# Spreading the modulation products over both products of a feed-forward block

## The chip, the cores and the metric

The kernel runs on one core of one Trainium2 chip. The metric is device time in microseconds (us) of one execution. A profile of one execution of the kernel before is read throughout; in it the span is counted from the first to the last instruction of the core.

## What is computed

A two-layer backbone over 256 latent tokens and 256 context tokens of width 1024. Each layer is a SwiGLU feed-forward block, a pair of token mixers, and a second feed-forward block; each of the three is wrapped in norms that are modulated by vectors computed from a conditioning vector:

```python
for l in range(DEPTH):                                   # DEPTH = 2
    mod = (silu(c) @ w_ada[l] + b_ada[l])                # 9 vectors of 1024 for the latent tokens
    mod_c = (silu(c_ctx) @ w_ada[l] + b_ada[l])          # 9 for the context tokens
    x = add_residual(x, swiglu(modulate(x, nw[0], mod[0], mod[1]), ffn_w_in[l, 0], ffn_w_out[l, 0]), nw[1], mod[2], 0.5)
    ...                                                  # the same for the context tokens, then the mixers
    x = add_residual(x, swiglu(modulate(x, nw[4], mod[6], mod[7]), ffn_w_in[l, 1], ffn_w_out[l, 1]), nw[5], mod[8], 0.5)

def swiglu(h, w_in, w_out):                              # w_in 1024 x 5632, w_out 2816 x 1024
    a, b = split(h @ w_in, 2)
    return (silu(a) * b) @ w_out
```

The "modulation products" are the rows of `silu(c) @ w_ada`. In this kernel they aren't matmuls: w_ada lies transposed, and each product is a multiply-and-sum on VectorE.

## The kernel before, in words

All matrix products are done on TensorE as three passes (`mm3`, L280 to L283): each operand is split into a high and a low part (`split`, L112 to L117: a cast on ScalarE, L115, then a subtraction on VectorE, L116), and high x high, high x low and low x high are summed.

A feed-forward block (`ffn`, L288) has two loops. The first product (`fin`) runs over 22 column blocks f of 128 hidden units. For each it loads 1 MB of weights as two tiles `raw` of 512 KB (`load`, L104; issued by SyncE, L108), splits each into a tile `w`, does 8 x 2 x 3 = 48 matmuls (L281 to L283) over 512 token columns, and evaluates silu(a)*b into `g` (`fin_ev`, L305 to L309: ScalarE L307, VectorE L308). The second product (`fout`) runs over 11 pairs of hidden blocks; for each it loads two `raw` tiles again, splits them, splits two `g` tiles into `gs` (L354 and L355), and does 48 matmuls with 512 output columns. In the last feed-forward block only the 256 latent tokens are left.

The modulation products run beside these loops. One step of the generator `ada_gen` (L127 to L137) loads two `raw` tiles of w_ada and does, for each tile and each of the two conditions, one multiply-and-sum on VectorE (L133): four VectorE instructions a step, two where only the latent condition is left. `pump` (L139) takes steps of a chain of such generators. In the first feed-forward block of a layer the chain has 24 steps: a gate (4), a shift and a scale (8), a gate (4), a shift and a scale (8). In the second of layer 0 it has 12, in the last one 4. At the end of a gate, small VectorE instructions (L185, L186) finish it and GpSimd writes it to DRAM (L188, `scr`), from where it is read back later (L194). The conditions silu(c) lie in the tiles `cs`, two of the 15 slots that `g` is taken from too.

Four `raw` tiles exist for all loads: fin, fout and w_ada share them in turn. Five `w` tiles exist, that is two and a half blocks of split weights. The order on each engine is set by a scheduler that goes by the order of the program and by when it expects operands to be ready; SyncE issues its loads in one order, VectorE and ScalarE do theirs in one order, and an instruction that waits holds those behind it on its engine.

In the loop before, the steps are dealt out over the f loop of the first product alone (L333 to L335): 24 steps over 20 f, that is one step behind each f and two behind every fifth.

Of the kernel before, what the change touches and what calls it, by code (L numbers as in the profile page):

```python
# [24 lines left out]
NF = FF // P  # L25
# [7 lines left out]
def build(ctx, tc, a):  # L33
# [34 lines left out]
    slots = Ring(rp, "r", 15)  # L68

    def bank():  # L70
        return banks.get([P, 512])

    def slot(shape, dt=F32):
        return slots.get(shape, dt)
# [4 lines left out]
    def tmp2(shape=(P, 512), dt=F32):  # L79
        return t2.tile(list(shape), dt, tag="t2", name="t2")  # L80
# [23 lines left out]
    def load(src, halves=(0, 1)):  # L104
        rs = []
        for j in halves:
            r = rawp.tile([P, 1024], F32, tag="raw", name="raw")
            nc.sync.dma_start(r, src[:, j * 1024:(j + 1) * 1024])  # L108
            rs.append(r)
        return rs  # L110

    def split(src, pin=False):  # L112
        keep = tc.keep_in_program_order if pin else (lambda z: z)
        w = wp.tile([P, 2, 1024], F32R, tag="w", name="w")
        keep(nc.scalar.copy(w[:, 0, :], src))  # L115
        keep(dve.tensor_tensor(out=w[:, 1, :], in0=src, in1=w[:, 0, :], op=ALU.subtract))  # L116
        return w  # L117

    cs = {}

    def load_cs(conds):
        for c in conds:
            cs[c] = slot([P, D])
            nc.sync.dma_start(cs[c], a["cc"][c].partition_broadcast(P))
            tc.keep_in_program_order(act(cs[c], cs[c], AF.Silu))
# [13 lines left out]
    def pump(g, n=1):  # L139
        for _ in range(n):  # L140
            if next(g, 1) == 1:
                return
# [75 lines left out]
    def norm_xn(c, alloc):  # L218
        xs = []
        for j in range(2):  # L220
            t = 2 * c + j
            ss = small(2, "ss")
            for hf in range(2):
                junk = jp.tile([P, 512], BF16, tag="ja", name="ja")
                act(junk, X[t][:, hf * 512:(hf + 1) * 512], AF.Square, accum_out=ss[:, hf:hf + 1])  # L225
            r = rstd_2(ss)
            xn = alloc([P, D])
            dve.tensor_scalar(out=xn, in0=X[t], scalar1=r, scalar2=None, op0=ALU.mult)
            xs.append(xn)
        return xs  # L230

    def norm_q(c, q, xs, AB, h):
        A, B = AB
        bk = bank()
        b = bk.rearrange("p (k n) -> p k n", k=2)
        for kk in range(2):
            k = 2 * q + kk
            for j in range(2):
                nc.tensor.transpose(b[:, kk, j * P:(j + 1) * P], xs[j][:, k * P:(k + 1) * P], ident)  # L239
        hf = tmp2([P, 2, 256])  # L240
        for kk in range(2):
            k = 2 * q + kk
            act(hf[:, kk, :], b[:, kk, :], AF.Identity, bias=B[:, c, k:k + 1], scale=A[:, c, k:k + 1])
        banks.put(bk)
        hH = h[q][:, :, 0, c * 256:(c + 1) * 256]
        dve.tensor_copy(hH, hf)  # L246
        dve.tensor_tensor(out=h[q][:, :, 1, c * 256:(c + 1) * 256], in0=hf, in1=hH, op=ALU.subtract)
# [32 lines left out]
    def mm3(o, wH, wL, xH, xL, start, stop):  # L280
        mm(o, lhsT=wH, rhs=xH, start=start, stop=False)  # L281
        mm(o, lhsT=wH, rhs=xL, start=False, stop=False)  # L282
        mm(o, lhsT=wL, rhs=xH, start=False, stop=stop)  # L283

    def fin_w(l, i, f, halves=(0, 1), pin=False):
        return [split(r, pin) for r in load(a["fin"][l, i, f], halves)]

    def ffn(l, i, st, AB, fetch, pairs, side, nside, after=None, out=None, xctx=None):  # L288
        h, w01 = st
        NT = 2 * len(pairs)  # L290
        N = 256 * len(pairs)
        g = {}

        def fin_mm(fs, ws, abs_, c0, c1):
            for k in range(KD):
                for f in fs:
                    wt = ws[f][k // 4].rearrange("p s (k n) -> p s k n", k=4)
                    for z in range(2):
                        lw = wt[:, :, k % 4, z * P:(z + 1) * P]
                        mm3(abs_[f][z][:, c0:c1], lw[:, 0], lw[:, 1], h[k // 2][:, k % 2, 0, c0:c1],  # L300
                            h[k // 2][:, k % 2, 1, c0:c1], k == 0, k == KD - 1)

        def fin_ev(f, ab):
            if f % 2 == 0:
                g[f // 2] = slot([P, 2, 512])  # L305
            sg = tmp2()
            act(sg[:, :N], ab[0][:, :N], AF.Silu)  # L307
            dve.tensor_tensor(out=g[f // 2][:, f % 2, :N], in0=ab[1][:, :N], in1=sg[:, :N], op=ALU.mult)  # L308
            banks.put(*ab)  # L309

        f0 = 0
        if len(pairs) == 2:
            if w01 is None:
                w01 = [fin_w(l, i, 0), fin_w(l, i, 1)]
            ab01 = [[bank(), bank()], [bank(), bank()]]
            fin_mm((0, 1), w01, ab01, 0, 256)
            xs = xctx or norm_xn(CTX, tmp4)
            for q in range(4):
                norm_q(CTX, q, xs, AB, h)
            if xctx:  # L320
                slots.put(*xctx)
            fin_mm((0, 1), w01, ab01, 256, 512)
            for f in range(2):
                fin_ev(f, ab01[f])
            f0 = 2
        load_cs(pairs)
        done = 0
        for f in range(f0, NF):
            w = fin_w(l, i, f, pin=False)
            ab = [bank(), bank()]  # L330
            fin_mm((0,), [w], [ab], 0, N)
            fin_ev(f, ab)
            want = (f + 1 - f0) * nside // (NF - f0)  # L333
            pump(side, want - done)
            done = want  # L335
        for _ in side:
            pass
        slots.put(*cs.values())
        cs.clear()

        y = [[bank(), bank()] for _ in range(NT)]
        NP = NF // 2

        def fout_w(f2):
            r = load(a["fout"][l, i, f2])
            ws = [split(r[0]), split(r[1])]
            if f2 < NP - 2:
                gt = hp.tile([P, 2, 2, 512], F32R, tag="h", name="gs")
                gs = [gt[:, 0], gt[:, 1]]
            else:  # L350
                gs = [slot([P, 2, 512], F32R) for _ in range(2)]
            for j in range(2):
                gsrc = g[f2][:, j, :N]
                nc.scalar.copy(gs[j][:, 0, :N], gsrc)  # L354
                dve.tensor_tensor(out=gs[j][:, 1, :N], in0=gsrc, in1=gs[j][:, 0, :N], op=ALU.subtract)  # L355
            slots.put(g[f2])
            return ws, gs

        def fout_mm(t, j, ws, gs, start, stop, halves=(0, 1)):
            gH = gs[j][:, 0, t * P:(t + 1) * P]  # L360
            gL = gs[j][:, 1, t * P:(t + 1) * P]
            for hf in halves:
                cs_ = slice(hf * 512, (hf + 1) * 512)
                mm3(y[t][hf], gH, gL, ws[j][:, 0, cs_], ws[j][:, 1, cs_], start, stop)

        for f2 in range(NP - 2):
            ws, gs = fout_w(f2)
            for j in range(2):
                for t in range(NT):
                    fout_mm(t, j, ws, gs, f2 == 0 and j == 0, False)  # L370
        tail = [fout_w(NP - 2), fout_w(NP - 1)]
        Gb = fetch()
        for t in range(NT):
            for hf in range(2):
                for e in range(2):
                    for j in range(2):
                        fout_mm(t, j, tail[e][0], tail[e][1], False, e == 1 and j == 1, (hf,))
            post_norm(t, y[t], Gb, out)
            if t == 1 and after is not None:
                after()  # L380
        slots.put(*tail[0][1], *tail[1][1], *Gb.values())
# [617 lines left out]
```

## Time and profile before

| | |
|---|---|
| time, median of 3 runs | 2244.57 us (2239.93 to 2246.06) |
| span of the profiled execution | 2238.5 us |
| from the start of the last work in the chain (2234.64 us) to the span's end | 3.9 us |
| PE busy | 2179.3 us (97%) |
| DVE busy | 1377.6 us (62%) |
| ACT busy | 859.2 us (38%) |
| bytes moved | 307.34 MB, mean 137 GB/s |

The profile gives the profiled execution by its span alone; it lies 1.4 us under the fastest and 6.1 us under the median of the timed runs. In the profile, PE is TensorE's matmul, PEld its weight load, DVE is VectorE, ACT ScalarE, POOL GpSimd, SP SyncE; SPq and POOLq are the issues of DMAs. PEclk is the granted TensorE clock as a share of 2.4 GHz. The four feed-forward blocks lie in the trace at about 24 to 413 us (layer 0, first), 945 to 1301 us (layer 0, second), 1315 to 1670 us (layer 1, first) and 2043 to 2235 us (the last).

### The profile page before, as it was taken

The page shows a single profiled execution, that of the slowest core. Times are in us where ns is not written, and L with a number is a line of the kernel's source. Part 1 is how long each engine was busy: PE and PEld are TensorE (multiplying, and loading weights), DVE is VectorE, ACT ScalarE, POOL GpSimd, SP SyncE. Part 2 cuts the span into 40 slices and gives each one's busy share as a digit, 9 for nine tenths or more (in the row PEclk, how much of TensorE's full clock was granted, in tenths as well). Part 3 has the DMA queues.
Part 4 walks back from the last instruction along what each step waited for, and adds up shares of the span by engine and source line. Part 5 has one row for each costly group of instructions (what it writes and reads, how often), then busy time and mean ns, then how long its engine had stood idle before and what let it go on. Part 6 is the DMA issues. An engine that isn't in the chain of part 4 may idle for free. (4 is left out here: it accounts for less than half of the span.)

```text
span 2238.5 us, 32969 instructions
## 1 busy us (share of the span) xinstructions
PE 2179.3 (97%) x13280; PEld 1936.9 (87%) x13280; DVE 1377.6 (62%) x2234; ACT 859.2 (38%) x1379; POOL 134.9 (6%) x249
## 2 busy tenths in 40 slices
PE   7999999999999999999999999999999999998998
PEld 4887778799999999888888888888879999997997
DVE  3786662586767665565644268746338767766564
ACT  3221242555445432432223252223236545445443
POOL 1000000200100000100000020000011000001000
PEclk9999999999999999999999999999999999999999
DMA  7665552122122223255544327667322322445673
GB/s 297 188 225 162 197 170 94 66 79 89 54 88 67 71 91 116 67 169 151 170 141 133 102 69 207 217 203 235 102 68 97 121 80 93 141 142 168 221 216 123
DMA packets 85546, 307.34 MB, mean 137 GB/s; under 512 B 10416, under 2 KB 10544, under 8 KB 85392
## 3 DMA queue, kind: packets, MB, share of 16 engines
q1 hardware_dynamic: 82224, 295.87, 40.7%
q0 software_dynamic: 2880, 8.31, 1.4%
q8 instruction: 104, 1.70, 0.3%
q10 hardware_dynamic: 288, 1.05, 0.1%
q14 instruction: 50, 0.41, 0.1%
HBM read 304.10 MB, written 1.09 MB: 136 GB/s over the span
## 5 line engine op out<-in xcount | busy, mean ns | idle before, releaser
L115 ACT CAST w<-raw 128x1024 fp32r<-128x1024 f32 x408 | 427.4, 1051 | 833.0 <-PE ps L283 470.7
L116 DVE TENSOR_TENSOR w<-raw,w 128x1024 fp32r<-128x1024 f32 x408 | 497.0, 1221 | 399.8 <-ACT w L115 398.9
L283 PE MATMUL ps<-h,w 128*128 128x256 f32 (+1 forms) x2176 | 718.9, 331 | 9.2 <-DVE w L116 9.1
L281 PE MATMUL ps<-h,w 128*128 128x256 f32 (+1 forms) x2176 | 717.5, 331 | 3.7 <-DVE h L246 2.9
L282 PE MATMUL ps<-h,w 128*128 128x256 f32 (+1 forms) x2176 | 718.5, 331 | 0.0
L283 PEld LDWEIGHTS ps<-h,w 128*128 128x128 f32 x2176 | 413.5, 190 | 52.2 <-DVE w L116 12.3
L281 PEld LDWEIGHTS ps<-h,w 128*128 128x128 f32 x2176 | 412.8, 190 | 43.0 <-DVE h L246 4.0
L282 PEld LDWEIGHTS ps<-h,w 128*128 128x128 f32 x2176 | 413.9, 190 | 40.3 <-DVE w L116 0.8
L133 DVE CUSTOM_DVE_ANT_0 jd<-raw,r 128x1024 bf16<-128x1024 f32 x224 | 273.6, 1222 | 161.1 <-DMA raw<-wada_dram 157.8
L281 PE MATMUL ps<-w,h 128*128 128x256 f32 x1088 | 308.9, 284 | 0.0
L282 PE MATMUL ps<-w,h 128*128 128x256 f32 x1088 | 308.1, 283 | 0.0
L283 PE MATMUL ps<-w,h 128*128 128x256 f32 x1088 | 307.8, 283 | 0.0
L281 PEld LDWEIGHTS ps<-w,h 128*128 128x128 f32 x1088 | 208.6, 192 | 0.4
L282 PEld LDWEIGHTS ps<-w,h 128*128 128x128 f32 x1088 | 208.7, 192 | 0.3
L283 PEld LDWEIGHTS ps<-w,h 128*128 128x128 f32 x1088 | 208.6, 192 | 0.0
L281 PE MATMUL ps<-w,gs 128*128 128x512 f32 x504 | 197.4, 392 | 2.5 <-ACT gs L354 2.5
L282 PE MATMUL ps<-w,gs 128*128 128x512 f32 x504 | 197.3, 391 | 0.0
L283 PE MATMUL ps<-w,gs 128*128 128x512 f32 x504 | 197.2, 391 | 0.0
L281 PEld LDWEIGHTS ps<-w,gs 128*128 128x128 f32 x504 | 95.3, 189 | 22.8 <-ACT gs L354 2.9
L283 PEld LDWEIGHTS ps<-w,gs 128*128 128x128 f32 x504 | 95.3, 189 | 20.5 <-DVE gs L355 0.7
L282 PEld LDWEIGHTS ps<-w,gs 128*128 128x128 f32 x504 | 95.3, 189 | 19.7
L307 ACT ACTIVATE t<-ps 128x512 f32<-128x512 f32 (+1 forms) x88 | 47.6, 541 | 115.8 <-PE ps L283 115.8
(166 smaller groups left out, 2131.3 us busy)
## 6 DMA issues: line engine op xcount, KB each, us to landing
raw<-fin_dram SPq DMA_DIRECT2D x176, 512.0 KB, 4.3
raw<-wada_dram SPq DMA_DIRECT2D x128, 512.0 KB, 4.6
raw<-win_dram SPq DMA_DIRECT2D x128, 512.0 KB, 3.6
raw<-fout_dram SPq DMA_DIRECT2D x88, 512.0 KB, 3.6
r<-wada_dram SPq DMA_DIRECT2D x16, 512.0 KB, 10.2
raw<-wout_dram SPq DMA_DIRECT2D x16, 512.0 KB, 3.5
r<-scr POOLq DMA_DIRECT2D x10, 512.0 KB, 4.8
r<-cc_dram SPq DMA_DIRECT2D x7, 512.0 KB, 5.0
```

The costliest lines, as they stand in the source:

```text
L115: keep(nc.scalar.copy(w[:, 0, :], src))
L116: keep(dve.tensor_tensor(out=w[:, 1, :], in0=src, in1=w[:, 0, :], op=ALU.subtract))
L133: dve.tensor_tensor_reduce(out=junk, in0=r[j], in1=cs[c], scale=1.0, scalar=0.0, op0=ALU.mult, op1=ALU.add, accum_out=out[:, c, 2 * u + j: ...
L281: mm(o, lhsT=wH, rhs=xH, start=start, stop=False)
L282: mm(o, lhsT=wH, rhs=xL, start=False, stop=False)
L283: mm(o, lhsT=wL, rhs=xH, start=False, stop=stop)
L307: act(sg[:, :N], ab[0][:, :N], AF.Silu)
```

## The change

The steps of the chain are dealt out over the f loop of the first product and over the first 9 of the 11 pairs of the second, and the chain is drained, and the `cs` slots are given back, behind that second loop. The count per call is rounded up, against a denominator that is two short of the loops' total length less one, so the chain is through one call before the last. For 24 steps there are 29 calls and a denominator of 28, and 18 steps come in the first product and 6 in the second; no call takes two.

```diff
         load_cs(pairs)
-        done = 0
+        NP = NF // 2
+        done = [0, 0]
+
+        def pump_to_here():
+            done[0] += 1
+            want = min(nside, -(-done[0] * nside // (NF - f0 + NP - 3)))
+            pump(side, want - done[1])
+            done[1] = want
+
         for f in range(f0, NF):
             w = fin_w(l, i, f, pin=False)
             ab = [bank(), bank()]
             fin_mm((0,), [w], [ab], 0, N)
             fin_ev(f, ab)
-            want = (f + 1 - f0) * nside // (NF - f0)
-            pump(side, want - done)
-            done = want
-        for _ in side:
-            pass
-        slots.put(*cs.values())
-        cs.clear()
+            pump_to_here()
...
             for j in range(2):
                 for t in range(NT):
                     fout_mm(t, j, ws, gs, f2 == 0 and j == 0, False)
+            pump_to_here()
+        for _ in side:
+            pass
+        slots.put(*cs.values())
+        cs.clear()
         tail = [fout_w(NP - 2), fout_w(NP - 1)]
```

The order of the instructions on TensorE and on GpSimd is the same in both kernels; on ScalarE one cast in each of three feed-forward blocks stands a few places later. VectorE and SyncE are reordered inside the feed-forward blocks only.

On SyncE, in the first product of the first feed-forward block, this stood at the third place where two steps came behind one f (raw are the load tiles, fin_dram the weights of the first product, wada_dram those of the modulation):

```order
L108 DMA raw_1633<-fin_dram 128x1024
L108 DMA raw_1635<-fin_dram 128x1024
L108 DMA raw_1696<-wada_dram 128x1024
L108 DMA raw_1698<-wada_dram 128x1024
L108 DMA raw_1708<-fin_dram 128x1024
L108 DMA raw_1710<-fin_dram 128x1024
L108 DMA raw_1778<-wada_dram 128x1024
L108 DMA raw_1780<-wada_dram 128x1024
L108 DMA raw_1790<-wada_dram 128x1024
L108 DMA raw_1792<-wada_dram 128x1024
L108 DMA raw_1802<-fin_dram 128x1024
L108 DMA raw_1804<-fin_dram 128x1024
```

And this stands in the changed kernel in the same product, some blocks on, at one of the two places where a call takes no step:

```order
L108 DMA raw_1579<-wada_dram 128x1024
L108 DMA raw_1581<-wada_dram 128x1024
L108 DMA raw_1591<-fin_dram 128x1024
L108 DMA raw_1593<-fin_dram 128x1024
L108 DMA raw_1654<-fin_dram 128x1024
L108 DMA raw_1656<-fin_dram 128x1024
L108 DMA raw_1724<-wada_dram 128x1024
L108 DMA raw_1726<-wada_dram 128x1024
L108 DMA raw_1736<-fin_dram 128x1024
L108 DMA raw_1738<-fin_dram 128x1024
```

The four loads of w_ada in a row are gone; loads of the two kinds alternate in pairs, and now and then two pairs of fin follow each other.

On VectorE, at the change from the first to the second product of the first feed-forward block, the order before was (L133 the modulation products, L116 the subtraction for a weight tile w, L308 the end of a block of the first product, L355 the split of g into gs, where two steps' products still stand ahead of it):

```order
L133 ISA jd_2189,adar_362<-raw_2181,r5_612 128x1024
L170 TENSOR_TENSOR adaB_365<-adar_362,bada_99 128x8 x2
L308 TENSOR_TENSOR r1_1937<-ps3_1964,t2_2013 128x512
L116 TENSOR_TENSOR w_2209<-raw_2205,w_2209 128x1024
L355 TENSOR_TENSOR r9_2783<-r1_1937,r9_2783 128x512
L116 TENSOR_TENSOR w_2212<-raw_2207,w_2212 128x1024
L308 TENSOR_TENSOR r2_2088<-ps5_2039,t2_2089 128x512
L116 TENSOR_TENSOR w_2272<-raw_2268,w_2272 128x1024
L355 TENSOR_TENSOR r4_2798<-r2_2088,r4_2798 128x512
L355 TENSOR_TENSOR gs_2215<-r3_602,gs_2215 128x512 x2
L116 TENSOR_TENSOR w_2275<-raw_2270,w_2275 128x1024
```

In the changed kernel the same place reads (L356 is L355 of before):

```order
L116 TENSOR_TENSOR w_2131<-raw_2127,w_2131 128x1024
L356 TENSOR_TENSOR r9_2783<-r1_1871,r9_2783 128x512
L133 ISA jd_2257,adar_363<-raw_2253,r4_609 128x1024
L116 TENSOR_TENSOR w_2134<-raw_2129,w_2134 128x1024
L133 ISA jd_2259,adar_363<-raw_2253,r5_612 128x1024
L308 TENSOR_TENSOR r2_2022<-ps5_1973,t2_2023 128x512
L133 ISA jd_2261,adar_363<-raw_2255,r4_609 128x1024
L116 TENSOR_TENSOR w_2194<-raw_2190,w_2194 128x1024
L133 ISA jd_2263,adar_363<-raw_2255,r5_612 128x1024
L356 TENSOR_TENSOR gs_2137<-r3_602,gs_2137 128x512 x2
L356 TENSOR_TENSOR r3_2798<-r2_2022,r3_2798 128x512
```

The four products of one step (raw_2253 and raw_2255) now stand among the splits of the first weight tiles of the second product (w_2131, w_2134, w_2194) and ahead of its first gs; before, no product came behind the last evaluation but one.

## Rows read from the trace of the kernel before

**Rows 1.** The page's first line on the engines: busy time, share of the span, instructions.

```profile
PE 2179.3 (97%) x13280; PEld 1936.9 (87%) x13280; DVE 1377.6 (62%) x2234; ACT 859.2 (38%) x1379; POOL 134.9 (6%) x249
```

**Rows 2.** What TensorE's matmuls waited for in the whole span: line, releaser, us in total, times, longest.

```profile
PE ps L239 <- DVE t L228: 16.7, 12, 6.2
PE ps L894 <- DMA r<-wada_dram: 10.1, 2, 9.9
PE ps L283 <- DVE w L116: 9.1, 6, 5.0
...
PE ps L281 <- ACT gs L354: 2.5, 1, 2.5
```

**Rows 3.** The same view for 60 to 300 us (first feed-forward block) and for 1339 to 1660 us (the first of layer 1).

```profile
PE ps L283 <- DVE w L116: 7.4, 3, 5.0
...
PE ps L283 <- DVE w L116: 1.2, 1, 1.2
```

**Rows 4.** Busy time by stretch, in the columns of the view (us, then PE, PEld, DVE, ACT, POOL busy with counts, granted clock, DMA share, GB/s): the two stretches of half clock in the first feed-forward block, one behind it, and a like place behind the second block.

```profile
222.60:229.40 6.80, 5.39 (x13) 4.23 (x14) 6.73 (x11) 0.00 (x0) 0.00 (x0) 0.50 0.60 198
297.70:304.50 6.80, 6.46 (x15) 4.64 (x16) 6.80 (x11) 6.80 (x12) 1.12 (x2) 0.50 0.82 256
417.20:420.60 3.40, 3.40 (x15) 3.21 (x16) 1.52 (x4) 2.65 (x6) 0.00 (x0) 0.50 0.00 0
...
936.00:943.00 7.00, 6.52 (x36) 5.38 (x37) 4.21 (x8) 4.40 (x11) 1.64 (x4) 1.00 0.00 0
```

**Rows 5.** The same view by stage: first product of the second block of layer 0; both products of the first block of layer 0, of the second of layer 0, and of the first of layer 1; both of the last block.

```profile
972.00:1189.00 217.00, 217.00 (x958) 179.65 (x958) 125.15 (x177) 61.77 (x73) 2.99 (x4) 1.00 0.51 161
...
66.00:400.00 334.00, 323.97 (x1399) 265.26 (x1398) 212.12 (x315) 86.41 (x105) 4.69 (x6) 0.98 0.55 173
972.00:1287.00 315.00, 315.00 (x1391) 260.80 (x1391) 155.71 (x209) 87.84 (x104) 2.99 (x4) 1.00 0.45 146
1339.00:1656.00 317.00, 315.77 (x1393) 261.13 (x1393) 183.00 (x262) 85.94 (x104) 3.89 (x5) 1.00 0.57 182
2045.00:2221.00 176.00, 176.00 (x1275) 167.56 (x1274) 103.62 (x130) 83.21 (x112) 1.55 (x2) 1.00 0.62 198
```

**Rows 6.** Counts in the first product of the first block: weight splits on VectorE (L116) since 56 us, and last the matmuls since 66 us (us, busy and count, granted clock, DMA share, GB/s).

```profile
56.00:98.00 42.00, 12.22 (x10) 1.00 0.60 199
...
56.00:208.00 152.00, 33.32 (x28) 1.00 0.64 200
56.00:218.00 162.00, 34.16 (x28) 1.00 0.64 195
...
66.00:218.00 152.00, 152.00 (x674) 1.00 0.65 199
```

**Rows 7.** In order of time: VectorE's and SyncE's work from 189 to 201 us, one cycle with one step, then what stands around 207 to 223 us (start, duration, engine, line, operation; in brackets the idle time before and its releaser).

```profile
189.19 1.23 DVE L133 CUSTOM_DVE_ANT_0 jd<-raw,r 128x1024 bf16<-128x1024 f32 x1 [3.68 <-DMA raw<-wada_dram]
...
195.74 1.47 SPq L108 DMA_DIRECT2D raw<-wada_dram  x2
...
200.40 1.23 DVE L133 CUSTOM_DVE_ANT_0 jd<-raw,r 128x1024 bf16<-128x1024 f32 x1 [3.55 <-DMA raw<-wada_dram]
...
207.50 1.76 POOL L188 DMA_DIRECT2D scr<-adag  x2 [106.30 <-DVE adag L186]
209.12 1.05 ACT L115 CAST w<-raw 128x1024 fp32r<-128x1024 f32 x1 [1.85 <-DMA raw<-fin_dram]
...
215.22 1.23 DVE L133 CUSTOM_DVE_ANT_0 jd<-raw,r 128x1024 bf16<-128x1024 f32 x1 [6.39 <-DMA raw<-wada_dram]
...
221.58 1.22 DVE L133 CUSTOM_DVE_ANT_0 jd<-raw,r 128x1024 bf16<-128x1024 f32 x1 [3.26 <-DMA raw<-wada_dram]
222.74 1.22 DVE L116 TENSOR_TENSOR w<-raw,w 128x1024 fp32r<-128x1024 f32 x1
```

**Rows 8.** SyncE's issues from 200 to 232 us.

```profile
202.93 3.21 SPq L108 DMA_DIRECT2D raw<-fin_dram  x2
206.95 17.36 SPq L108 DMA_DIRECT2D raw<-wada_dram  x4
225.12 2.87 SPq L108 DMA_DIRECT2D raw<-fin_dram  x2
```

**Rows 9.** What ended the idle time of engines: for 66 to 296 us (first product of the first block) two lines, then for 298 to 400 us (its second product) one.

```profile
ACT w L115 <- DMA raw<-fin_dram: 129.6, 29, 19.6
DVE jd L133 <- DMA raw<-wada_dram: 45.8, 15, 6.4
...
ACT w L115 <- PE ps L283: 71.8, 18, 4.4
```

**Rows 10.** Groups of VectorE instructions by line and shape (count | busy us, mean ns of one | idle before), then DMA issues with KB and the median us from issue to landing.

```profile
L116 DVE TENSOR_TENSOR w<-raw,w 128x1024 fp32r<-128x1024 f32 x408 | 497.0, 1221 | 399.8 <-ACT w L115 398.9
L133 DVE CUSTOM_DVE_ANT_0 jd<-raw,r 128x1024 bf16<-128x1024 f32 x224 | 273.6, 1222 | 161.1 <-DMA raw<-wada_dram 157.8 <-ACT r L125 0.3
L308 DVE TENSOR_TENSOR r<-ps,t 128x512 f32<-128x512 f32 x66 | 45.3, 686 | 32.8 <-PE ps L283 26.3 <-ACT t L307 6.4
...
L355 DVE TENSOR_TENSOR gs<-r,gs 128x512 fp32r<-128x512 f32 x54 | 34.5, 684 | 0.4 <-ACT gs L354 0.4
...
raw<-fin_dram SPq DMA_DIRECT2D x176, 512.0 KB, 4.3
scr<-adag POOLq DMA_DIRECT2D x10, 4.0 KB, 10.1
```

More of the change, by code (lines that the diff above doesn't have):

```diff
@@ L332, in ffn @@
             fin_ev(f, ab)
-            want = (f + 1 - f0) * nside // (NF - f0)
-            pump(side, want - done)
-            done = want
-        for _ in side:
-            pass
-        slots.put(*cs.values())
-        cs.clear()
+            pump_to_here()
         y = [[bank(), bank()] for _ in range(NT)]
-        NP = NF // 2
         def fout_w(f2):
```

## The prediction

> **What bounds the kernel now.** I read the engines' busy times first: TensorE is busy 97% of the span and no other engine above 62% [rows 1]. So a change that leaves TensorE's instructions and their order alone can win only what TensorE waits, and what it loses at half clock behind a wait. Next I read its waits [rows 2]: the largest two lie at norms and at the start, away from the change. The third and the fourth are the ones to look at: matmuls that wait for a split weight tile (9.1 us in 6 waits) and one that waits for the first gs of a second product (2.5 us). By stretch, 7.4 us of the 9.1 lie in the first feed-forward block and 1.2 in the first of layer 1 [rows 3]. Then the granted clock: it stands at 0.50, which is 1.2 instead of 2.4 GHz, for 6.80 us from 222.60 and for 6.80 us from 297.70 [rows 4], both right behind these waits.
>
> A check by counts: 958 matmuls in 217.00 us of undisturbed first product are 0.2265 us each, and a block of 48 takes 10.87 us [rows 5]. At that rate the 1399 matmuls of the first block's two products need 316.9 us, and they took 334; the 1393 of layer 1's first need 315.5 and took 317; the second block of layer 0 took exactly its 315, and in the last block the engine is busy without a gap [rows 5]. So 17.1 + 1.5 = 18.6 us is all that these four stages have to give.
>
> Why the first block starves can be seen by counting. Each split tile serves 24 matmuls, 5.43 us. By 98 us 10 tiles were split, which lasts until 66 + 10 x 5.43 = 120.3 us: a lead of 22.3. By 208 us 28 were split, lasting until 218.1: a lead of 10.1. At 218 there were still 28, and TensorE had started 674/24 = 28.1 [rows 6]. So splits came every 110/9 = 12.2 us per block where TensorE takes 10.87. The reason is not VectorE's work, which is 4 x 1.22 + 2 x 1.22 + 0.69 = 8.0 us for a block with one step [rows 10]. It is the loads: four raw tiles are shared, the w_ada pair can be issued only when the tiles ahead of it are used, and VectorE stands still until it lands. A cycle with one step runs from the product at 189.19 to that at 200.40, 11.21 us: 6.5 us of work, then 195.74 to 200.40, 4.66 us, from issue to landing [rows 7]. ScalarE's casts there wait for fin loads (129.6 us), while in the second product, with no step beside it, they wait for TensorE to free w tiles (71.8 us): there the supply is ahead [rows 9].
>
> Two things make a cycle worse. Two steps behind one f put four w_ada loads in a row on SyncE's queue: fin loads issued at 202.93 are followed by fin loads only at 225.12 [rows 8]. And the gate's write to DRAM at 207.50 has, by its two small tiles, a landing time of 10.1 us [rows 10]; the next products waited 6.39 and 3.26 us for their loads instead of 3.55 [rows 7], 6.1 us more. A weight tile cast by 210.2 was subtracted at 222.74 only, because products stood ahead of it [rows 7].
>
> **The change part by part.** No instruction is added or removed.
>
> *The double steps go.* In the first product 18 steps stand over 20 f instead of 24, none double. I price the supply by the cycle of 11.21 us, plus 6.1 for a gate's write. A block without a step saves between 0 (it has no row here) and 5.8 us (fin's landing of 4.3 us [rows 10] and one cast of 1.05 [rows 7] would make 5.4). The critical place is the second gate, about 13 blocks behind 98 us: 13 x 11.21 + 6.1 = 151.8, less 0 to 11.6 for two blocks without a step, against 13 x 10.87 = 141.3 of TensorE. The lead goes from 22.3 to between 11.8 and 23.4. The next tile then comes after 7.8 us (a cycle less the 3.4 us between two tiles of a pair, which I estimate from two products and a subtraction of 1.22 each less overlap) plus 6.1, that is 13.9. So TensorE waits 0 to 2.1 us; I take 0, since the lower end holds only if a block without a step saved nothing. Saved: 7.4 us of waits and 6.80/2 = 3.4 at half clock.
>
> *The transition.* Before, products of two last steps kept VectorE full up to the end of the first product, so the evaluation and gs came late: 2.5 us and another 3.4 at half clock, 6.80/2. Now one step stands there, 4 x 1.22 = 4.9 us, and its loads come behind those of the second product's first two pairs. The first gs needs TensorE to be through a quarter of the last block, some 8 us before its end; behind that stand at most two products and one split, 3.7 us. I count 5.9 us saved. If the cover is gone, a wait like the old one is the price.
>
> *The second product.* A pair with a step costs VectorE 4.9 + 2.4 + 2 x 0.68 = 8.7 us of 10.87. A cycle there is 11.21 + 1.37 - 0.69 = 11.9 us, so six of them in eight pairs eat 6 x 1.0 = 6.2 us of lead and the other two restore it. The lead entering is about that at the gate less 6, 6 to 17 us: cost 0, at worst a wait of a few us. The last loads of the tail have no w_ada among them, and A and B of the next norm come a pair before the tail.
>
> *Layer 1's first block*: 1.2 us of wait saved; the other two blocks, nothing, for they have no wait to lose and fewer products. The `cs` slots held longer cost nothing: nine g slots come free meanwhile.
>
> The sum: 7.4 + 3.4 + 2.5 + 3.4 + 1.2 = 17.9 us, under the 18.6 of the counts. Against the profiled 2238.5 us that gives 2220.6; the median of the timed runs lies 6.1 us above the profiled span, and I keep that distance: 2244.6 - 17.9 = 2226.7, said as 2227. If those 6.1 us are further waits of the same kind, they go too: 2220.
>
> The Trainium skill (DMA: Bandwidth & Descriptors, Anatomy of one DMA) gives a fixed 2.0 us plus bytes over 436 GB/s for a DMA, on GpSimd's path; an estimate from that page for 512 KB is 3.2 us. By it a cycle would be 9.7 us, under TensorE's 10.87, and no lead would be lost at all with single steps; the traced 4.66 us contradict it, and the sum keeps the row.
>
> **The rivals.**
>
> *A small wait stays (R1).* The lead is at its lower end at the second gate or in the second product: one wait of 2.1 us and 3.4 at half clock. For it: both gates still write to DRAM beside the loads. Gain 17.9 - 5.5 = 12.4, time 2232.
>
> *The supply was slow anyway (R2).* If single cycles take the mean of 12.2 us rather than 11.21, 13 blocks take 158.6 + 6.1 (less 0) against 141.3; even without adding the gate the lead falls to 22.3 - 17.3 = 5.0, the wait is 13.9 - 5.0 = 8.9 and the half clock 3.4. Gain 17.9 - 12.3 = 5.6, time 2239, which is no change to a measurement here. For it: the w_ada waits are in 15 places [rows 9]. Against: the mean holds the double steps and one gate.
>
> *The wait at the transition spreads (R3).* On VectorE products now stand ahead of the first gs in three of the four blocks, and an in-order engine that waits there for a w_ada load holds gs, and so TensorE. Price 2.5 + 3.4 = 5.9 us each; with a second such wait among the pairs behind it in each, 3 x 11.8 = 35.4, of which the first block already pays 5.9. Against the 12.0 us saved in the first products that is slower by 17.5, 2262; with only one a block, 3 x 5.9 - 12.0 - 5.9 is nothing. It decides from a lead under about 6 us at the end of the first product. Against it: the blocks outside the first have leads that no wait touched [rows 5].
>
> TensorE's clock gives a band, not a case. The norm behind the first block was followed by half clock for 3.40 us from 417.20, the same norm behind the second by none [rows 4]. The Trainium skill (TensorE: Matmul & The Clock Gate, What's actually happening) says that the gate's watch runs free of the kernel, so shifting the stages by 18 us may put a pause elsewhere in it; the rows agree that like places differ. With 1.7 us for 3.40 at half clock, three such places are plus or minus 5 us.
>
> **How the numbers follow.** Forecast 0.52, R1 0.23, R2 0.15, R3 0.10. A difference under 0.3%, 6.7 us, can't be told from none here. Forecast and R1 are faster (0.75, and a little of R2's spread makes 0.76), R2 is mostly no change (0.14), R3 slower (0.10). The range goes from 2217 (2220 with some of the clock's band) to 2241, just over R2's time; outside it lie R3 and a little below.
>
> **What would show it.** Right: the first block's two products take about 317 us for their 1399 matmuls with no wait for w in the first product, no half clock inside them, SyncE never four w_ada loads in a row; in the second product VectorE is busier and ScalarE's casts no longer wait only for TensorE. R1 and R2: a wait for w near the second gate's write, R2 several before it. R3: waits for gs or w behind the transition in more than one block. Wrong altogether: the wait for w gone and the time the same, which would mean that TensorE's pace and not its waits had hidden the difference.

## The result, and the profile after

The spread kernel is slower: 2259.41 us median (2254.63 to 2260.66) against 2244.39 us, ratio 1.0069 with a 95% interval of 1.0052 to 1.0085. Of all timed runs below one, of 6431.92 us in E9, is left out of its median. The profiled execution has a span of 2258.9 us, 20.4 us more than before. TensorE's instructions are the same and so is their busy time but for the half clock; the page's first line, beside [rows 1]:

```profile
PE 2182.8 (97%) x13280; PEld 1939.1 (86%) x13280; DVE 1376.4 (61%) x2234; ACT 859.3 (38%) x1379; POOL 134.7 (6%) x249
```

So some 17 of the 20 us are waits, and 3.5 are half clock. TensorE's waits in the whole span, the lines that answer to [rows 2] (L356 is L355 of before):

```profile
PE ps L283 <- DVE gs L356: 14.0, 2, 8.4
PE ps L283 <- DVE w L116: 10.8, 8, 5.8
...
PE ps L281 <- DVE r L308: 4.4, 2, 3.9
```

The wait for the first gs, 2.5 us once, has become 14.0 us in two; a wait for r, the evaluation of the last block of a first product, is new; the waits for w are about as long as before, but lie elsewhere. Where, the view by stage shows (columns as in [rows 5]): first product and second product of layer 0's first block, both products of layer 0's second block, then the two of layer 1's first block.

```profile
66.00:287.00 221.00, 217.93 (x961) 179.79 (x960) 144.96 (x221) 56.38 (x66) 3.56 (x4) 1.00 0.56 178
287.00:397.00 110.00, 101.14 (x434) 82.84 (x433) 65.54 (x95) 29.85 (x38) 1.12 (x2) 0.95 0.49 168
969.00:1284.00 315.00, 315.00 (x1392) 260.84 (x1391) 156.05 (x209) 88.01 (x104) 2.99 (x4) 1.00 0.44 146
1336.00:1563.70 227.70, 220.41 (x963) 180.90 (x962) 132.41 (x195) 56.22 (x66) 2.76 (x3) 0.99 0.55 173
1563.70:1675.70 112.00, 102.41 (x434) 83.75 (x434) 50.77 (x67) 29.86 (x38) 1.11 (x2) 0.95 0.47 163
```

At 0.2265 us a matmul the counts of the two first blocks need 217.7, 98.3, 218.1 and 98.3 us. So layer 0's first product now loses 3.3 us, its second product 11.7; layer 1's lose 9.6 and 13.7. Layer 0's second block has no gap, though its steps are spread too. Before, the two blocks together lost 17.1 and 1.5 us [rows 5]. Layer 0's block is about where it was, with its loss moved from the first product to the second; the 20 us come from layer 1's, which had almost nothing to gain. In both the change of products was followed by half clock, and in layer 1 a wait in the first product too:

```profile
291.40:301.60 10.20, 5.45 (x13) 4.29 (x14) 8.69 (x13) 4.87 (x8) 0.00 (x0) 0.50 0.51 178
1537.20:1544.00 6.80, 3.27 (x8) 2.60 (x9) 2.97 (x4) 1.04 (x1) 0.00 (x0) 0.50 0.52 172
1567.90:1574.70 6.80, 4.68 (x11) 3.76 (x12) 4.31 (x6) 4.10 (x8) 0.00 (x0) 0.50 0.45 155
1581.60:1585.00 3.40, 3.40 (x10) 2.62 (x9) 2.06 (x4) 1.04 (x1) 0.55 (x1) 0.50 0.62 193
```

What held gs is seen in VectorE's, ScalarE's and SyncE's work around the end of layer 0's first product, which ends at 287 us (order of time; in brackets the idle time before and its releaser):

```profile
281.17 0.33 SPq L108 DMA_DIRECT2D raw<-wada_dram  x1
...
284.15 1.14 ACT L355 CAST gs<-r 128x512 fp32r<-128x512 f32 x2
...
285.64 1.23 DVE L133 CUSTOM_DVE_ANT_0 jd<-raw,r 128x1024 bf16<-128x1024 f32 x1 [3.90 <-DMA raw<-wada_dram]
286.80 1.22 DVE L116 TENSOR_TENSOR w<-raw,w 128x1024 fp32r<-128x1024 f32 x1
287.93 1.22 DVE L133 CUSTOM_DVE_ANT_0 jd<-raw,r 128x1024 bf16<-128x1024 f32 x1
288.05 0.33 SPq L108 DMA_DIRECT2D raw<-wada_dram  x1
289.08 0.69 DVE L308 TENSOR_TENSOR r<-ps,t 128x512 f32<-128x512 f32 x1
291.97 1.22 DVE L133 CUSTOM_DVE_ANT_0 jd<-raw,r 128x1024 bf16<-128x1024 f32 x1 [2.21 <-DMA raw<-wada_dram]
293.12 1.22 DVE L116 TENSOR_TENSOR w<-raw,w 128x1024 fp32r<-128x1024 f32 x1
294.26 1.22 DVE L133 CUSTOM_DVE_ANT_0 jd<-raw,r 128x1024 bf16<-128x1024 f32 x1
295.40 1.29 DVE L356 TENSOR_TENSOR gs<-r,gs 128x512 fp32r<-128x512 f32 x2
```

The high part of gs was cast by 285.3 us. Its low part had to wait behind four products, and these behind their loads: the step's first w_ada tile landed at 285.64; the second could be issued only at 288.05, when the weight split of 286.80 had freed a raw tile, and landed at 291.97. From the first of the four products to gs VectorE needed 9.76 us, 2.21 of them idle for the second load while gs stood ready, and it could begin only 1.5 us before TensorE was through with the first product, after 3.90 us of idle time for the first load. The prediction had counted two products and one split, 3.7 us, behind the point where gs can be done; four products, two splits and an evaluation (L308) stood there, and two load times with them.

The same pattern slows VectorE in layer 1's first product. There a step has only two products in the later part of the chain. First VectorE before, at about 1461 us, with SyncE's issue; then the spread kernel at 1503 us:

```profile
1456.12 1.46 SPq L108 DMA_DIRECT2D raw<-wada_dram  x2
...
1461.69 1.23 DVE L133 CUSTOM_DVE_ANT_0 jd<-raw,r 128x1024 bf16<-128x1024 f32 x1 [4.46 <-DMA raw<-wada_dram]
...
1463.44 1.21 DVE L133 CUSTOM_DVE_ANT_0 jd<-raw,r 128x1024 bf16<-128x1024 f32 x1
...
1472.02 1.23 DVE L133 CUSTOM_DVE_ANT_0 jd<-raw,r 128x1024 bf16<-128x1024 f32 x1 [5.09 <-DMA raw<-wada_dram]
```

```profile
1503.41 1.23 DVE L133 CUSTOM_DVE_ANT_0 jd<-raw,r 128x1024 bf16<-128x1024 f32 x1 [4.48 <-DMA raw<-wada_dram]
1504.56 1.22 DVE L116 TENSOR_TENSOR w<-raw,w 128x1024 fp32r<-128x1024 f32 x1
1504.67 0.33 SPq L108 DMA_DIRECT2D raw<-wada_dram  x1
1507.87 1.23 DVE L133 CUSTOM_DVE_ANT_0 jd<-raw,r 128x1024 bf16<-128x1024 f32 x1 [2.09 <-DMA raw<-wada_dram]
...
1515.36 1.23 DVE L133 CUSTOM_DVE_ANT_0 jd<-raw,r 128x1024 bf16<-128x1024 f32 x1 [4.52 <-DMA raw<-wada_dram]
```

Before, both tiles of a step were issued together and both products stood in a row: one landing a cycle, 10.33 us from step to step, under TensorE's 10.87 us a block. Now products and weight splits alternate, the second tile is issued only at 1504.67, right behind the first tile's product, and a cycle has two landings in a row: 11.95 us here, and 11.4 to 14.0 in the four cycles from 1476.56 to 1526.77 us, over 10.87. Such cycles use up the lead of the split weights. That they are enough for a wait is not shown by this: E9 below has them too, and no wait for w.

### The profile page after: what moved, and what is told of

The parts are those of the page before. It is cut to its first block, busy times and chain, and to the rows that moved or that the text cites. A ratio compares the mean times of both kernels' runs of the same rounds, so it can differ in the third digit from the quotient of the medians.

```text
span 2258.9 us, 32961 instructions
## 1 busy us (share of the span) xinstructions
PE 2182.8 (97%) x13280; PEld 1939.1 (86%) x13280; DVE 1376.4 (61%) x2234; ACT 859.3 (38%) x1379; POOL 134.7 (6%) x249
## 2 busy tenths in 40 slices
DMA packets 85546, 307.34 MB, mean 136 GB/s; under 512 B 10416, under 2 KB 10544, under 8 KB 85392
## 5 line engine op out<-in xcount | busy, mean ns | idle before, releaser
L116 DVE TENSOR_TENSOR w<-raw,w 128x1024 fp32r<-128x1024 f32 x408 | 497.4, 1221 | 310.1 <-ACT w L115 309.2
L133 DVE CUSTOM_DVE_ANT_0 jd<-raw,r 128x1024 bf16<-128x1024 f32 x224 | 273.7, 1222 | 261.9 <-DMA raw<-wada_dram 258.5
## 6 DMA issues: line engine op xcount, KB each, us to landing
r<-wada_dram SPq DMA_DIRECT2D x16, 512.0 KB, 10.2
```

Source lines behind the costliest of these rows:

```text
L133: dve.tensor_tensor_reduce(out=junk, in0=r[j], in1=cs[c], scale=1.0, scalar=0.0, op0=ALU.mult, op1=ALU.add, accum_out=out[:, c, 2 * u + j: ...
```

## Experiments

Three theories were put against each other: A, that products stand ahead of gs on VectorE; B, that the steady alternation is slow wherever it stands; C, that the four raw tiles shared by weights and w_ada are the root, since each kind's loads wait for the other's use. Later D, on the gates' write to DRAM. The kernel before was run beside them (2241 to 2242 us median).

**E1, steps held back at the change of products.**

```diff
-            pump_to_here()
+            if f2 == 2:
+                done[0] = done[1]
+            if f2 >= 3:
+                want = min(nside, done[0] - (-(f2 - 2) * (nside - done[0]) // (NP - 5)))
+                pump(side, want - done[1])
+                done[1] = want
```

> The spread kernel, but no step is taken behind the first three pairs of the second product; what is left (6 of 24 steps) is dealt out behind pairs 3 to 8. Theory A (a step's products stand on VectorE ahead of the first gs of the second product and hold it for two load times): the waits for gs (14.0 us in 2) and the 4.4 us for r at the change of products go, with some 13 us at half clock behind them; time about 2259 - 14 - 4 - 6 = 2235. Theory B (the steady alternation of one step and one block is itself too slow, wherever the steps stand): the waits move into the later pairs and the time stays within 5 us of 2259.

Measured: 2233.56 us, ratio to before 0.9964 (0.9952 to 0.9977): faster than both. TensorE's waits at the places in question:

```profile
PE ps L283 <- DVE w L116: 7.0, 4, 5.0
```

No wait for gs is left, and 0.4 us for r. So the loss in the second products came from where the steps stood, as A says, and not from steps in a second product as such: six of them ran there without a wait. B falls for the second products. 5.0 us of wait for w stay in layer 1's first product.

**E2, gs of the first pair in slots of its own.**

```diff
-            if f2 < NP - 2:
+            if 0 < f2 < NP - 2:
...
+            if f2 == 0:
+                slots.put(*gs)
```

> The spread kernel, but the gs of the first pair of the second product is kept in two free slots, so that it need not wait for the first product to be through with h and is split long before. Theory A: the first wait at the change of products in the first feed-forward block (8.4 us) falls to what the second pair's gs is late, some 2 to 3 us one block later, and likewise in layer 1; time about 2245. Theory B: no gs wait, but waits for w take its place; time above 2254.

Measured: 2263.24 us in one run, no better, and by neither theory: the gs waits went, the waits for w stayed as they were (10.3 us), and a third wait came in their place:

```profile
PE ps L281 <- DVE r L308: 24.5, 3, 12.2
```

In layer 0 the first pair's early matmuls ran, and the fourth token tile then waited 12.2 us for its bank of results (`ps`), which the last evaluation (L308) frees; that stood on VectorE behind products that waited for their loads. A named the wrong victim: it isn't gs alone that is late, but whatever stands behind a product that waits for its load.

**E3 and E4, load tiles apart from the four raw tiles for w_ada, in the spread kernel and in the kernel before.** Each step takes the two slots anew from the ring of 15 that `g` is taken from, whichever are free, so loads of several steps can be under way.

```diff
-            r = load(a["wada"][l, m * 4 + u])
+            r = [slot([P, D]) for _ in range(2)]
+            for j in range(2):
+                nc.sync.dma_start(r[j], a["wada"][l, m * 4 + u][:, j * D:(j + 1) * D])
...
+            slots.put(*r)
             yield
```

> The spread kernel, but the loads of w_ada go into two slots of their own instead of the four raw tiles, so they no longer wait for weight tiles to be used, nor these for them. Theory C (the root is the sharing of four raw tiles: w_ada loads are issued late and VectorE stands still with w and gs behind): the waits for w in the first products and for gs and r all go, nothing at half clock inside the feed-forward blocks; time 2222 to 2230. Rival (VectorE's order alone, products ahead of gs, whatever the loads do): the change of products still waits 5 us or more in two blocks, time above 2240.

> The kernel before (steps packed into the first product) with the same own slots for the w_ada loads. Theory C: its waits for w (9.1 us) go too, about 2226 to 2232, the same as the spread kernel with own slots within 5 us, so the spread is worth nothing once the loads are apart. Rival (the double steps' work on VectorE, 4 x 4 x 1.22 us, is the cause): some 5 us of wait for w stay in the first feed-forward block, 2235 to 2240.

Measured: 2221.65 us, ratio 0.9918 (0.9903 to 0.9932), and 2221.11 us, ratio 0.9916 (0.9902 to 0.9931). In E3 both first blocks run at TensorE's pace without a gap or half clock:

```profile
68.00:383.50 315.50, 315.50 (x1394) 261.26 (x1393) 212.09 (x315) 87.93 (x104) 4.69 (x6) 1.00 0.55 176
1321.00:1636.50 315.50, 315.50 (x1395) 261.28 (x1394) 184.56 (x262) 88.15 (x104) 3.89 (x5) 1.00 0.53 167
```

In E4 TensorE waits for w, gs or r nowhere in the first blocks either. So C's forecast came true, and the rival about double steps falls: four double steps cost nothing there, and the spread is worth nothing either. These two are the fastest kernels here, 20 us under before. But the edit changed more than the sharing. The steps ran ahead: in E3 the modulation products beside layer 0's first product were all done at 207 us, and none stood ahead of gs at the change to the second, where the spread kernel has four:

```profile
205.80 1.22 DVE L135 CUSTOM_DVE_ANT_0 jd<-r,r 128x1024 bf16<-128x1024 f32 x1
...
278.36 1.29 DVE L359 TENSOR_TENSOR gs<-r,gs 128x512 fp32r<-128x512 f32 x2 [1.06 <-ACT gs L358]
...
285.06 1.22 DVE L135 CUSTOM_DVE_ANT_0 jd<-r,r 128x1024 bf16<-128x1024 f32 x1
```

So these two runs show that the losses of both kernels go when w_ada has tiles besides the four. Whether that is for tiles apart, for more tiles, or for the order that follows from them isn't told apart; no run gave all loads six shared tiles, or two fixed ones to w_ada. The rival of E3, VectorE's order alone, was not put to the test by it.

**E5, the spread in layer 1's first block only** (a flag `spread = (l, i) == (1, 0)` chooses the rule of each block).

> The spread is used only in the first feed-forward block of layer 1; the other blocks deal their steps out as before. By the two traces that block took 22.6 us more with the spread (8.6 in the first product, 14.0 from there to the end of the second), and the first block of layer 0 2.0 us less. Theory C (loads shared, so products wait twice a cycle there) has it as a matter of each block by itself: ratio 1.009 to 1.011, about 2264 against 2242. Rival (the loss in layer 1 was carried over from what came before, or a chance of that run): within 0.3%.

Measured: 2264.38 us, ratio 1.010 (1.008 to 1.012). The loss belongs to that block by itself.

**E6 and E7, half the products, or half the loads.**

```diff
-                for c in conds:
+                for c in conds[:1]:
...
+                if len(conds) == 2:
+                    dve.tensor_copy(out[:, 1, 2 * u + j:2 * u + j + 1], out[:, 0, 2 * u + j:2 * u + j + 1])
```

```diff
-            r = load(a["wada"][l, m * 4 + u])
+            r = load(a["wada"][l, m * 4 + u], (0,)) * 2
```

> The spread kernel with all loads of w_ada, but only the latent condition's products; the context's vectors are copied from them, so half of the modulation is left out where there are two conditions. This takes up to 2.4 us of VectorE's work out of each step and no load. Theory C: the waits for w, gs and r stay (over 15 us in all), time above 2245. Rival (VectorE's work is what comes late): they fall under 5 us, time about 2225.

> The spread kernel with all products, but the second w_ada tile of each step is not loaded and the products read the first tile again, so half of the modulation's rows are wrong copies. This takes a load and its landing time out of each cycle and no work from VectorE. Theory C: the waits for w, gs and r fall under 8 us, time 2222 to 2236. Rival (VectorE's work): they stay over 15 us, time above 2245.

Measured: 2256.06 and 2234.45 us, one run each. TensorE's waits, of E6 and then of E7:

```profile
PE ps L285 <- DVE gs L358: 12.9, 2, 6.6
...
PE ps L283 <- DVE r L310: 9.1, 2, 4.7
```

```profile
PE ps L281 <- DVE r L308: 4.1, 1, 4.1
PE ps L283 <- DVE gs L356: 3.5, 1, 3.5
```

Taking away VectorE's work left 22 us of wait at the changes of products (18.4 in the spread kernel); taking away one load of two left 7.6, all in layer 0. VectorE's work is not what comes late; the loads are. (In E6 layer 1's first product ran without a wait worth naming, 0.2 us: its order on VectorE differs too, so that part is not told apart.)

**E8, E1's rule in layer 0's first block only.**

> The late steps of e1 only in the first feed-forward block of layer 0; the others as before. By the trace of e1 that block gains 14.8 us, and layer 1's first product, which lost 5.5 us there, keeps the time of before: about 2242 - 15 = 2227, ratio 0.993 to 0.994. Rival: the gain of e1 came from elsewhere, ratio above 0.996.

Measured: 2225.88 us, ratio 0.9927 (0.9901 to 0.9952), as expected. This is what the idea is worth with shared tiles: spread where the loop is overfull, away from the change of products, and not where there was no wait.

**E9 and E10, the gate written to DRAM in adjacent places**, in the spread kernel and in the kernel before.

```diff
-                pool.dma_start(scr[c].rearrange("(k p) -> p k", p=P), G[:, c, :])
+                pool.dma_start(scr[c].rearrange("(p k) -> p k", p=P), G[:, c, :])
```

> The spread kernel, but each gate is written to DRAM in runs of eight numbers per partition instead of single numbers to scattered places (so its channels come back in another order and the gates are wrong). Theory D (the scattered write holds up the loads beside it by about 6 us, the price in the prediction): the waits right behind the gates' writes go, 6.2 us in layer 1 and 2.4 to 3.6 in layer 0, with the half clock behind the first; the waits at the changes of products stay; time 2244 to 2250. Rival (the pair of w_ada loads is late there for want of tiles, as everywhere): the waits stay, within 4 us of 2259.

> The kernel before with the same gate write in whole runs (its gates are wrong too). Theory D: the 5.0 us wait behind the second gate and the half clock behind it go, and the lead stays longer; 2228 to 2235 against 2242. Rival (the double step alone): within 4 us of 2242.

Measured: 2235.77 us, ratio 0.9978 (0.9966 to 0.9989), and 2228.10 us, ratio 0.9939 (0.9916 to 0.9962). E10 lies 14 us under before, at the lower end of what was expected. E9 lies some 20 us under the spread kernel (0.9978 against 1.0069, each beside its own runs of the kernel before), more than expected. The write's time to landing in E10, against the 10.1 us of [rows 10], and the products behind the second gate, against [rows 7]:

```profile
scr<-adag POOLq DMA_DIRECT2D x10, 4.0 KB, 4.0
```

```profile
205.58 1.07 POOL L188 DMA_DIRECT2D scr<-adag  x2 [103.38 <-DVE adag L186]
```

```profile
209.42 1.23 DVE L133 CUSTOM_DVE_ANT_0 jd<-raw,r 128x1024 bf16<-128x1024 f32 x1 [2.50 <-DMA raw<-wada_dram]
```

The product behind the gate waited 2.50 us and the next not at all, where before they waited 6.39 and 3.26. In E9 both first products run without a wait for w. Theory D holds, and it reaches further than it was given: the waits at the changes of products were expected to stay, and of their 18.4 us 6.9 are left, none of them for gs:

```profile
PE ps L281 <- DVE r L308: 6.9, 2, 5.0
```

Yet the order there is that of the spread kernel. In layer 0 the same four products stand ahead of gs, with two loads to wait for:

```profile
272.97 1.23 DVE L133 CUSTOM_DVE_ANT_0 jd<-raw,r 128x1024 bf16<-128x1024 f32 x1 [3.56 <-DMA raw<-wada_dram]
...
279.12 1.23 DVE L133 CUSTOM_DVE_ANT_0 jd<-raw,r 128x1024 bf16<-128x1024 f32 x1 [2.04 <-DMA raw<-wada_dram]
...
282.56 1.29 DVE L356 TENSOR_TENSOR gs<-r,gs 128x512 fp32r<-128x512 f32 x2
```

From the first of them to gs it is 9.6 us, as in the spread kernel (9.8). But VectorE begins 10.5 us before TensorE is through with the first product (at 283.49 us), where it began 1.5 us before; in layer 1 it is 10.5 against 2.8. So the order at the change makes a wait only where VectorE comes to it late, and the gates' writes are a large part of what made it late. The cycles with two landings are in E9 too: in layer 1 the five from 1452.99 to 1514.09 us take 11.9 to 12.5 us each, and TensorE waits for no w.

In the spread kernel the same shows at layer 1's gate, whose 5.8 us wait for w follows an idle time of 8.56 us on VectorE:

```profile
1523.79 0.88 POOL L188 DMA_DIRECT2D scr<-adag  x1 [151.62 <-DVE adag L186]
```

```profile
1537.70 1.23 DVE L133 CUSTOM_DVE_ANT_0 jd<-raw,r 128x1024 bf16<-128x1024 f32 x1 [8.56 <-DMA raw<-wada_dram]
```

The Trainium skill (Trainium Kernel Development and Optimization, Key Constraints) says that DMAs issued from different engines' queues run on the same 16 DMA engines and interleave. The runs fit this: the pattern of a 4 KB write on GpSimd's queue changed how late loads of 512 KB on SyncE's came.

## Why the prediction was wrong, point by point

*What there was to win* was right: 18.6 us by counts. E3 and E4 took 20 us off by removing these waits.

*The double steps* in layer 0 were nearly right: 0 to 2.1 us of wait were forecast for its first product, and it has 3.1 in two waits, the longest 2.0, with no half clock, where it had 7.4 and half clock. But the cycle was priced too low, 11.21 us from a single row: between 141.39 and 254.87 us seven cycles with one step take 11.6 to 12.2, 11.9 in the mean. The gates' writes were priced at 6.1 us each in kind rightly; E10, which keeps the double steps, takes 14 us off where E4 takes 21.

*The transition* is the step that failed. It read "behind that stand at most two products and one split, 3.7 us. I count 5.9 us saved". It priced VectorE's work, and too little of it, and not the loads that this work waits for, though the row for it was there: 4.66 us from issue to landing, and the rule that a w_ada load waits for a tile to be used. From the step's first product to gs it was 9.8 us. In its place stands a wait of 8.4 us and 10.2 us at half clock in layer 0, 5.6 + 3.9 and 6.8 + 3.4 in layer 1. A second error lies beneath: I carried the lead of the weight tiles, "6 to 17 us", over to the second product. That lead covers w. What counts for gs and for the last evaluation is how early VectorE comes to the step's products, and that was 1.5 and 2.8 us before the end of the first product. With 10.5 us (E9) gs came in time, and 1.9 and 5.0 us of wait for r were left.

*Layer 1's first block*, "1.2 us of wait saved", lost 8 us more in its first product and 14 more in its second. I took it as layer 0's with fewer products. But the new order waits for two landings a cycle where it was one, so half the products did not make a short cycle: 12.6 us in the mean of four, over 10.87. That spends the lead, and the gate's write came on top: the 5.8 us wait stands right behind it, and E9, with the same cycles, has none. E5 puts 22 us on this block alone.

*The rivals.* R3 had the mechanism, an in-order engine that waits for a w_ada load and holds gs, and its condition, a lead under about 6 us, was met, if it is taken as how early VectorE comes to the change (1.5 and 2.8 us). Its 2262 is near the 2259 measured, in part by luck: it had waits in three blocks, and layer 0's second has none. I gave it 0.10 because the other blocks' leads had been untouched, which says nothing of what the new order would leave of them. The forecast and R1 were wrong in sign. R2's slow cycle of 12.2 us was close in both layers (11.9 us in the mean in layer 0, 12.6 in layer 1's four); the time it forecast, 2239, left out the change of products.

## What to carry to other kernels

Before work that brings its own loads is moved beside another loop, count the landings in series that a cycle then has, and whose tile each load waits for; the work's own busy time says little. Where such a background stream shares tiles with the loads that bound the kernel, give it other tiles first: here that was worth 20 us, whichever way the steps were dealt out. Look at small writes beside the loads: adjacent places for the gate's write were worth 14 us before the change and some 20 after it, though a kernel that reads the gate back in the matching order was not run. And keep the stream away from places where the next consumer has little lead, the change of stages above all.

## What was not expected of the hardware

A 4 KB write to scattered places in DRAM took 10.1 us to land before and 11.2 in the spread kernel (medians), and 4.0 us to adjacent places (E9 and E10), with the same count of packets on the page (85546, of them 10416 under 512 B). The w_ada load issued beside the second gate's write was used 8.3 us after its issue before (206.95 to 215.22 us) and 4.4 us after it in E10 (205.04 to 209.42). That the writes cost 14 us of kernel time was somewhat more than the 12.2 us at which the two of layer 0's first block had been priced; the wait for w behind the second gate fell where the lead was already spent, and half clock followed. Why adjacent places land sooner with as many packets was not tried.
